# Differential attention: low parts of k in both halves of the rows, k in 512-token halves

## The chip, the cores and the metric

The kernel runs on one core of one Trainium2 chip. The time is device microseconds (us) of one execution; lower is better. The engines named below are TensorE (PE; its weight loads are listed apart as PEld), VectorE (DVE), ScalarE (ACT), GpSimd (POOL) and SyncE (SP, which issues DMAs).

## What is computed

Two blocks of two layers each on 1024 tokens with 1024 features, all in 32-bit floats. The change lies in the differential attention of the second block, which runs once per layer, so twice:

```python
q = q.reshape(B, S, DA_HEADS, 2, DA_QK_DIM).transpose(0, 2, 3, 1, 4)
k = k.reshape(B, S, DA_HEADS, 2, DA_QK_DIM).transpose(0, 2, 3, 1, 4)
...
s = jnp.einsum('bhmqd,bhmkd->bhmqk', q_blk, k).astype(jnp.float32) * scale
mask = kpos[None, :] <= qpos[:, None]
p = jax.nn.softmax(jnp.where(mask, s, -jnp.inf), axis=-1)
a = p[:, :, 0] - lam * p[:, :, 1]
return jnp.einsum('bhqk,bhkd->bhqd', a.astype(v.dtype), v)
```

There are 4 heads (DA_HEADS), each with two maps m of 64 features (DA_QK_DIM), and 8 query tiles of 128 tokens. Tile t sees the keys of tiles 0 to t.

## The kernel before, in words

**Products in parts.** A 32-bit operand is split into a high part (rounded to float32r) and a low part (the rest), and a product is the sum of high by high, low by high and high by low.

**The loop.** `diff_attention` (L1445) goes through n = 0 to 31, tile t = n % 8 of head n // 8. In one turn of the loop (L1607) the order on TensorE is written out and pinned: scores of map 0 of tile n; `values` of tile n-3 (L1572: weights times v); `transpose` of the first half of tile n-2 (L1561); `project` of q and k of tile n+3 (L1497: 24 products of 256 columns); scores of map 1 of tile n; `transpose` of the second half of tile n-2, if it has one; `turn` of tile n+2 (L1511: three transposes of q and k). The other engines take their instructions in an order that the scheduler sets when the program is built; each engine runs its own list strictly in that order.

**turn** puts the transposed, rotated q and k into SBUF. q of map m: high parts in rows 64 m and on, low parts in the other 64 rows (tile dq). k: high parts of both maps in both halves of the rows (tile dk, ScalarE, L1524). The low parts of k are in tile dkl, map m in rows 64 m (VectorE, L1529, two subtractions of 64x128). dk and dkl hold a head's 1024 tokens, with two buffers each.

**scores** (L1533) makes for each chunk of up to 512 keys two products with q of map m as weights: with dk over 128 rows, which sums high q by high k and low q by high k, and with dkl over the 64 rows of the map, high q by low k (L1547 and L1548). A last product of 128 columns adds the causal mask (weights and moving operand from the tile dccm, L1549). All score products of a map add up in one PSUM tile y of two buffers. VectorE then takes the negated maximum of each row (tile dnm, L1551), ScalarE the exponential (L1553), and after map 1 VectorE joins the two maps (L1555 to L1559).

**transpose and values.** The joined weights are turned by TensorE; ScalarE copies the high part, VectorE subtracts the low part (tiles dp, `split`, L191; one for the first four key tiles and one for the rest, one buffer each). `values` starts with the first dp tile; its ninth product is the first that reads the second one.

```python
1547  self.mm(sp[:, cs], q[:, m], kk[:, m, cs], start=True, stop=False)
1548  self.mm(sp[:, cs], q[r, m], kl[r, cs], start=False, stop=(c1 < W))
```

Every matrix product of the kernel is issued in the helper at L151 and every transposition by TensorE at L156, so the profile is read by tile names.

Of the kernel before, what the change touches and what calls it, by code (L numbers as in the profile page):

```python
# [12 lines left out]
F32 = mybir.dt.float32  # L13
F32R = mybir.dt.float32r
I32 = mybir.dt.int32
AF = mybir.ActivationFunctionType
OP = mybir.AluOpType
# [4 lines left out]
P = 128  # L22
# [75 lines left out]
class UT:  # L98
    """Transposed activations, split in two float32r parts: [feature, token]."""
# [12 lines left out]
class Pools:  # L112
    """Several pools, chosen by tag."""
# [8 lines left out]
class TagPool:  # L122
    """One pool per tag (a new pool waits only for the pools it overlaps); a tile without a tag is a tag of its own."""
# [18 lines left out]
class Kern:  # L142
# [30 lines left out]
    def psum(self, ctx, left="", right=""):  # L173
        """One PSUM pool per tag, stacked from either end."""
        for side, tags in (("left", left), ("right", right)):
            for t in tags:
                self.ps.tags[t] = self.pool(ctx, "ps" + t, space=PSUM, side=side)

    def pp(self, tag, bufs, shape=None):
        """PSUM tile; a tag of a phase always comes with the same bufs."""  # L180
        return self.ps.tile(shape or [P, 512], F32, tag=tag, bufs=bufs, name=self.nm(tag))
# [4 lines left out]
    def split(self, hi, lo, src, scale=None):  # L186
        """hi = float32r(src), lo = src - hi (src times scale), src in PSUM or SBUF."""
# [8 lines left out]
    def wsplit(self, hi, lo, raw, eng=None, cut=1, act=False):  # L196
        """Split, the high part on ScalarE if act; the low part in as many pieces as cut says (short ones delay other work
        of the engine less)."""
# [9 lines left out]
    def load_w(self, pool, w, c0, n, kts=KT, tag="w", bufs=None, dve=0, cut=1):  # L208
        """Weight columns c0..c0+n, split: w[kt][part] is [128, n]; every dve-th chunk on VectorE alone."""
# [15 lines left out]
    def next_w(self, c0, ahead=0):  # L225
        """The weight columns at c0 of the list in self.order, or those after them."""
# [7 lines left out]
    def gemm_T(self, w, ut, out, cols=slice(0, P)):  # L234
        """out [128 features, 1024 tokens] in PSUM, as two halves."""
        nc = self.nc
        for half in range(2):
            self.gemm_T_half(w, ut, half, out[half], cols)
# [7 lines left out]
    def gemm_N(self, ps, w, cols, lhs, kts=KT):  # L246
        """ps [128 tokens, features]; lhs(part, kt) is the stationary operand."""
# [7 lines left out]
    def transposes(self, dst, src, n):  # L255
        """dst [.., n, 128] = blocks of src [128, n * 128] transposed."""
# [3 lines left out]
    def to_T(self, src, ut, t):  # L260
        """src [128 tokens, 1024] in SBUF -> ut token tile t."""
# [6 lines left out]
    def rsqrt(self, y, v, pool, src=None, mul=1.0, eps=0.0):  # L268
        """y = v ** -0.5 (integer first guess, three Newton steps), v = src * mul + eps if src is given."""
# [20 lines left out]
    def silu2(self, out, src, tmp):  # L290
        """out = 2 silu(src) = src (1 + tanh(src / 2))."""
# [3 lines left out]
    def rms_rstd(self, src, n, eps, junk, pool):  # L295
        """[128, 1] = (mean(src ** 2) + eps) ** -0.5 over the free axis."""
# [13 lines left out]
    # ---------------------------------------------------------------- setup  # L310
# [11 lines left out]
    def transposed_columns(self, dst, rows_ap, nrow, pool):  # L322
        """dst [128, nrow] = rows_ap [nrow, 128] transposed."""
# [7 lines left out]
    # ---------------------------------------------------------------- first block, layer 0  # L331
    def phase_A(self, x_in):
        nc, i = self.nc, self.i
        with ExitStack() as ctx:
# [6 lines left out]
            with ExitStack() as c0:  # L341
# [23 lines left out]
                # relative position bias vectors, one row per head  # L365
# [11 lines left out]
                # shift and scale, one feature per partition  # L377
# [7 lines left out]
                # column c of block c: ones  # L385
# [69 lines left out]
            def fill(n):  # L455
                """PE work of the projections and gates, as many pieces."""
# [6 lines left out]
            def step(job, n):  # L463
                """The scores of job, with the rest of the one before it."""
# [42 lines left out]
    def dil_gate(self, lp, ut, w_in, hp, g, sgs):  # L507
        """2 silu(gate) of head pair hp of group g, transposed."""
# [13 lines left out]
    def dil_product(self, lp, hp, g, sgs, os, wtd, yT):  # L522
        """y^T rows of head pair hp of group g: attention times weight times gate."""
# [11 lines left out]
    def mod_jobs(self, lp, cs, jobs):  # L535
        """Thirds of silu(c) @ ada_w + ada_b of a layer, to DRAM, and the convolution taps by channel."""
# [63 lines left out]
    def dil_project(self, lp, ut, w_in, hp, g, res):  # L600
        """q, k, v of heads (2 hp, 2 hp + 1) of group g, tokens in the order of the group; v with tokens on
        partitions."""
# [30 lines left out]
        def split_q(q):  # L633
            """High parts of head a in rows 64 a, low parts in the others."""
# [8 lines left out]
        def split_k(k, low):  # L643
            """High parts of head a in both halves of the rows, low parts in rows 64 a."""
# [20 lines left out]
        # the second half of the tokens comes last in the very first group  # L665
# [13 lines left out]
    def dil_batches(self, lp, hp, g, tbd, std, qkv, os):  # L679
        """Unnormalised attention of heads (2 hp, 2 hp + 1) of group g -> os [2 heads x 64, token], as a list of  # L680
        batches."""
# [12 lines left out]
        class Head:  # L694
            def __init__(self, a):
# [7 lines left out]
                # batches of score tiles: rows, width, [(q0, k0, out position)], bias slices  # L703
# [24 lines left out]
            def finish(self):  # L728
                """Output row and row statistics, the latter to DRAM in token order."""
# [85 lines left out]
    def dil_weights(self, lp, hp, std, wtd):  # L815
        """exp(m_g - M) / sum_g s_g exp(m_g - M) per token, head, group."""
# [20 lines left out]
    # ---------------------------------------------------------------- first block, layer 1  # L837
    def rope_pairs(self, eng, a, b, cos, sin, pool, shp):
        """Rotate the pair (a, b) in place; cos and sin broadcast to shp."""
# [91 lines left out]
    def mla_heads(self, ctx, cr, lat, kbuf, rope, sgd, yT, rd, begin_tail):  # L931
# [60 lines left out]
        def scores(n):  # L992
            """exp(S - max) of query tile n % 8 of head n // 8."""
# [107 lines left out]
    def tail_weights(self, pool, w_out, kts, gate, eng, pin=False):  # L1101
        """Rows of w_out times the gate, split; eng multiplies."""
# [12 lines left out]
    def tail_begin(self, ctx, parts, w_out, layer, eng):  # L1115
        """First part of a tail, while the mixer still runs: the weights of its finished parts."""
# [8 lines left out]
    def tail_finish(self, ctx, early, late, w_out, x_res, layer):  # L1125
        """x = layernorm(alpha x + gate * (y @ w_out)); next layer's transposed input.

        Parts are the rows of y^T as [block, 128, token] views, in the order in which they are made."""
# [100 lines left out]
    # ---------------------------------------------------------------- second block, mixers  # L1229
    def phase_mix(self, l, ut, x_res):  # L1230
# [3 lines left out]
        with ExitStack() as ctx:  # L1234
# [35 lines left out]
            def end(early, n):  # L1270
                """Parts of the output product between the last tiles."""
# [12 lines left out]
    def pool_mixer(self, lp, us, pooled, sums, l, mixd):  # L1284
        """us [128 channels, 2, 1024 tokens]: windowed means minus us, times pool_w, to mixd."""
# [37 lines left out]
    def retention(self, lp, dp, wn, l, ut, w_in, mixd):  # L1323
        """Pool mixer and retention, to mixd; returns the last step of the latter, one tile at a time."""
# [120 lines left out]
    def diff_attention(self, dp, wn, l, ut, w_in, mixd, rest, late_pool, begin_tail, end, products):  # L1445
        """Differential attention of the four heads, one query tile after the other; the projections of q and k run
        LEAD tiles ahead."""
# [49 lines left out]
        def project(n):  # L1497
            """q and k of tile n % 8 of head n // 8, rotated."""
# [12 lines left out]
        def turn(n):  # L1511
            """Transposed and split. q: high parts of map m in rows 64 m, low parts in the others; k: high parts in both
            halves of the rows, low parts of map m in rows 64 m."""
            h, t = divmod(n, NT)
            c = raw_qk.pop(n)
            if t == 0:
                ks[h] = (lp.tile([P, 2, S], F32R, tag="dk", bufs=2, name=self.nm("dk")),
                         lp.tile([P, S], F32R, tag="dkl", bufs=2, name=self.nm("dkl")))
            kk, kl = ks[h]
# [3 lines left out]
            ts = slice(t * P, (t + 1) * P)  # L1523
# [4 lines left out]
            for m, r in enumerate(rows):  # L1528
                nc.vector.tensor_tensor(kl[r, ts], tp[r, 1 + m], kk[r, m, ts].bitcast(F32), OP.subtract)  # L1529
# [3 lines left out]
        def scores(n, m):  # L1533
            """exp(S_m - max); after both maps exp(S_0 - max) - lam z_0 / z_1 exp(S_1 - max), with the row sums z."""
            h, t = divmod(n, NT)
            W = (t + 1) * P
            q, (kk, kl) = qs[n], ks[h]
# [4 lines left out]
            r = slice(m * 64, (m + 1) * 64)  # L1542
# [375 lines left out]
```

## Time and profile before

| what | value |
|---|---|
| time, median of 3 runs | 4187.02 us (4184.1 to 4189.52) |
| span of the profiled execution, first to last instruction | 4168.8 us; its own total time is not listed apart |
| median less that span | 18.2 us |
| TensorE busy | 3945.4 us, 95% |
| weight loads busy | 3282.7 us, 79% |
| VectorE busy | 2430.4 us, 58% |
| ScalarE busy | 1371.7 us, 33% |
| GpSimd busy | 1087.9 us, 26% |
| the two attention loops, first scores to last maximum | 1776.8 to 1991.6 us and 3077.1 to 3291.9 us |

The profile is of one execution. Times within it are microseconds from the start of its span. A busy share over the whole span is a mean over stages with different limits, so the two attention loops are read by themselves. TensorE's products are pipelined and their ends are modelled, so that two neighbours can overlap in the list; what a product takes is read from one start to the next. Instructions on VectorE overlap a little in the same way.

### The profile page before, as it was taken

Reading aid. Unit: us, or ns where it says so; the run is one execution under the profiler, and the core shown is the slowest. Engines: PE = TensorE matmul, PEld = TensorE weight load, DVE = VectorE, ACT = ScalarE, POOL = GpSimd, SP = SyncE. Lnnn points to the kernel's source line nnn. Section 1 sums busy time; section 2 is a strip of 40 time slices with the busy share of each in tenths; the row PEclk is TensorE's granted clock in tenths of the full one; section 3 lists DMA queues with packets and bytes.
Section 4 is the critical chain, followed back from the end, with each engine's and each line's share of the span. In section 5 each row is a group of like instructions: output and inputs, shape, how many; then the busy total and the mean of one; then the engine's idle time right before and its main releaser. Section 6 shows DMA issues by size and latency. Waiting matters only on the chain. (4 is left out here: it accounts for less than half of the span.)

```text
span 4168.8 us, 54321 instructions
## 1 busy us (share of the span) xinstructions
PE 3945.4 (95%) x21085; PEld 3282.7 (79%) x21085; DVE 2430.4 (58%) x4606; ACT 1371.7 (33%) x2908; POOL 1087.9 (26%) x1016
## 2 busy tenths in 40 slices
PE   7989896899999889999999999997999999999998
PEld 5768775788888778988778888886988778888886
DVE  6545445947787767578753434438568764444436
ACT  3323331126777632255421111113235431111111
POOL 1111211410221322233133232324133222222233
PEclk9989998999999999999999999998999999999999
DMA  6363727320110243110421111113111231111112
GB/s 234 90 81 87 90 57 124 112 67 21 38 35 19 79 130 97 46 32 26 137 81 51 45 51 46 46 56 115 46 42 37 82 122 50 46 46 51 41 51 81
DMA packets 318896, 290.79 MB, mean 70 GB/s; under 512 B 70779, under 2 KB 273267, under 8 KB 318638
## 3 DMA queue, kind: packets, MB, share of 16 engines
q1 hardware_dynamic: 313362, 268.23, 23.8%
q10 hardware_dynamic: 5276, 19.08, 1.5%
q8 instruction: 167, 2.74, 0.3%
q14 instruction: 91, 0.75, 0.1%
HBM read 240.26 MB, written 51.72 MB: 70 GB/s over the span
## 5 line engine op out<-in xcount | busy, mean ns | idle before, releaser
L203 POOL TENSOR_TENSOR wl<-wr,wh 128x1024 fp32r<-128x1024 f32 (+1 forms) x253 | 497.9, 1977 | 1553.1 <-DVE wh L199 1458.8
L199 DVE CAST wh<-wr 128x1024 fp32r<-128x1024 f32 x222 | 180.2, 813 | 713.5 <-PE y L151 310.6
L151 PE MATMUL y<-uh_m,wl 128*128 128x512 f32 x1056 | 415.8, 394 | 4.7 <-DVE z L1643 4.2
L151 PE MATMUL y<-uh_m,wh 128*128 128x512 f32 x1056 | 418.6, 396 | 0.0
L151 PE MATMUL y<-ul_m,wh 128*128 128x512 f32 x1056 | 417.6, 395 | 0.0
L1796 ACT ACTIVATE cv<-y,cw 128x1024 f32<-128x1024 f32 x66 | 79.8, 1209 | 775.7 <-PE y L151 775.7
L151 PE MATMUL g<-uh_a,wl 128*128 128x512 f32 x568 | 234.8, 413 | 32.7 <-DVE sg L293 32.6
L151 PEld LDWEIGHTS y<-uh_m,wl 128*128 128x128 f32 x1056 | 198.2, 188 | 54.8 <-issue 4.6
L151 PEld LDWEIGHTS y<-uh_m,wh 128*128 128x128 f32 x1056 | 198.2, 188 | 48.2
L151 PEld LDWEIGHTS y<-ul_m,wh 128*128 128x128 f32 x1056 | 198.2, 188 | 47.5 <-DVE ul_m L191 0.9
L151 PE MATMUL g<-ul_a,wh 128*128 128x512 f32 x568 | 227.7, 401 | 0.5 <-POOL ul_a L422 0.4
L151 PE MATMUL g<-uh_a,wh 128*128 128x512 f32 x568 | 227.0, 400 | 0.0
L151 PE MATMUL y<-wo,yh 128*128 128x512 f32 x784 | 217.5, 400 | 2.7 <-ACT yh L1168 2.5
L191 DVE TENSOR_TENSOR pt<-t,pt 128x512 fp32r<-128x512 f32 x256 | 165.8, 680 | 21.9 <-ACT pt L190 21.0
L151 PEld LDWEIGHTS y<-wo,yh 128*128 128x128 f32 x784 | 147.7, 191 | 36.4 <-ACT yh L1168 4.3
L151 PE MATMUL y<-wl,hh 128*128 128x512 f32 x440 | 175.2, 398 | 0.0
L151 PE MATMUL y<-wh,hh 128*128 128x512 f32 x440 | 174.9, 398 | 0.0
L151 PE MATMUL y<-wh,hl 128*128 128x512 f32 x440 | 174.8, 397 | 0.0
L1005 DVE TENSOR_REDUCE nm<-s 128x1 f32<-128x1024 f32 x128 | 155.7, 1216 | 27.4 <-PE s L151 26.7
L151 PE MATMUL g<-wl,uh_n 128*128 128x256 f32 x576 | 166.2, 289 | 2.9 <-DVE dv L191 2.4
L151 PE MATMUL g<-wl,uh_f 128*128 128x256 f32 x576 | 166.0, 288 | 3.0 <-DVE dv L191 2.5
L151 PE MATMUL v<-pt,v 128*64 128x256 f32 (+1 forms) x1024 | 154.9, 294 | 10.2 <-DVE o L1040 10.2
(450 smaller groups left out, 10263.1 us busy)
## 6 DMA issues: line engine op xcount, KB each, us to landing
wr<-w_up SPq DMA_DIRECT2D x88, 512.0 KB
wr<-ada_w SPq DMA_DIRECT2D x48, 512.0 KB
wr<-w_down SPq DMA_DIRECT2D x44, 512.0 KB
wr<-a_w_in SPq DMA_DIRECT2D x36, 512.0 KB
wr<-w_in SPq DMA_DIRECT2D x24, 512.0 KB
xs<-wr SPq DMA_DIRECT2D x16, 512.0 KB
wr<-xs ACTq DMA_DIRECT2D x16, 512.0 KB
wr<-w_in SPq DMA_DIRECT2D x32, 256.0 KB
```

Source lines behind the costliest of these rows:

```text
L151: ins = self.nc.tensor.matmul(*args, **kw)
L191: nc.vector.tensor_tensor(lo, src, hi.bitcast(F32), OP.subtract)
L199: (self.nc.scalar.copy if act else self.nc.vector.tensor_copy)(hi, raw)
L203: (eng or self.nc.gpsimd).tensor_tensor(lo[..., cs], raw[..., cs], hi[..., cs].bitcast(F32), OP.subtract)
L1005: nc.vector.tensor_reduce(nm, sp, AX.X, OP.max, negate=True)
L1796: nc.scalar.activation(t, ps, AF.Identity, bias=cw[:, 3, c:c + 1], scale=cw[:, 2, c:c + 1])
```

## The change

The low parts of k are kept for both maps in both halves of the rows, as the high parts are. `turn` makes them with one subtraction of 128 rows by two maps by 128 tokens in place of two of 64x128. In `scores` the second product has 128 rows: it adds low q by low k to what was computed before. dk and dkl are split into halves of 512 tokens with three buffers each, in place of whole heads with two. Lines behind L1529 move up by two. Comments and docstrings that go are left out here.

```diff
 def turn(n):
     h, t = divmod(n, NT)
     c = raw_qk.pop(n)
-    if t == 0:
-        ks[h] = (lp.tile([P, 2, S], F32R, tag="dk", bufs=2, name=self.nm("dk")),
-                 lp.tile([P, S], F32R, tag="dkl", bufs=2, name=self.nm("dkl")))
-    kk, kl = ks[h]
+    if t % 4 == 0:
+        ks[h, t // 4] = [lp.tile([P, 2, 512], F32R, tag=x, bufs=3, name=self.nm(x)) for x in ("dk", "dkl")]
+    kk, kl = ks[h, t // 4]
...
-    ts = slice(t * P, (t + 1) * P)
+    ts = slice(t % 4 * P, (t % 4 + 1) * P)
     nc.scalar.copy(kk[:, :, ts], tp[:, 1:3])
...
-    for m, r in enumerate(rows):
-        nc.vector.tensor_tensor(kl[r, ts], tp[r, 1 + m], kk[r, m, ts].bitcast(F32), OP.subtract)
+    nc.vector.tensor_tensor(kl[:, :, ts], tp[:, 1:3], kk[:, :, ts].bitcast(F32), OP.subtract)
...
 def scores(n, m):
...
-    q, (kk, kl) = qs[n], ks[h]
+    q = qs[n]
...
-    r = slice(m * 64, (m + 1) * 64)
...
-        self.mm(sp[:, cs], q[:, m], kk[:, m, cs], start=True, stop=False)
-        self.mm(sp[:, cs], q[r, m], kl[r, cs], start=False, stop=(c1 < W))
+        kk, kl = ks[h, c0 // 512]
+        self.mm(sp[:, cs], q[:, m], kk[:, m, :c1 - c0], start=True, stop=False)
+        self.mm(sp[:, cs], q[:, m], kl[:, m, :c1 - c0], start=False, stop=(c1 < W))
```

The built programs have the same instructions on TensorE and SyncE, in the same order. On VectorE the list is rearranged by a few places. The first place is the stretch around the second maximum of tile 6 of the second head and the low part of the second dp tile of tile 4 behind it, which `values` of tile 4 reads (dnm: negated maxima; drr and rs: the norm of four finished tiles; dq: low parts of q). Before:

```order
L287 SCALAR_TENSOR_TENSOR rs_18585<-rs_18585,dss_18064 128x4
L1551 TENSOR_REDUCE dnm_18426<-y_18420 128x1
L191 TENSOR_TENSOR dp_18435<-t_18436,dp_18434 128x128
L1529 TENSOR_TENSOR dkl_18441<-t_18443,dk_18440 64x128 x2
L1531 TENSOR_TENSOR dq_18442<-t_18443,dq_18442 64x128 x2
L1555 RECIPROCAL drs_18349<-dsm_18348 128x2
L1551 TENSOR_REDUCE dnm_18462<-y_18456 128x1
```

With the change:

```order
L288 SCALAR_TENSOR_TENSOR drr_18569<-rs_18571,drr_18569 128x4
L1549 TENSOR_REDUCE dnm_18414<-y_18408 128x1
L191 TENSOR_TENSOR dp_18423<-t_18424,dp_18422 128x128
L1527 TENSOR_TENSOR dkl_18429<-t_18431,dk_18428 128x2x128
L1529 TENSOR_TENSOR dq_18430<-t_18431,dq_18430 64x128 x2
L1549 TENSOR_REDUCE dnm_18449<-y_18443 128x1
L1553 RECIPROCAL drs_18337<-dsm_18336 128x2
```

One short instruction of the norm (drr) now stands ahead of the maximum (dnm); the two subtractions for dkl have become one; and the next maximum stands ahead of the reciprocal (drs).

The second place is the next tile of the same head: the second maximum of tile 7 and the low part of the second dp tile of tile 5 (do with dcgs: the norm again). Before:

```order
L191 TENSOR_TENSOR dp_18484<-t_18485,dp_18483 128x512
L1601 SCALAR_TENSOR_TENSOR do_18063<-do_18063,drr_18583,dcgs 128x128 x2
L1551 TENSOR_REDUCE dnm_18556<-y_18550 128x1
L191 TENSOR_TENSOR dp_18565<-t_18566,dp_18564 128x256
L1529 TENSOR_TENSOR dkl_18441<-t_18572,dk_18440 64x128 x2
L1531 TENSOR_TENSOR dq_18571<-t_18572,dq_18571 64x128 x2
```

With the change:

```order
L191 TENSOR_TENSOR dp_18471<-t_18472,dp_18470 128x512
L1599 SCALAR_TENSOR_TENSOR do_18054<-do_18054,drr_18569,dcgs 128x128 x2
L1549 TENSOR_REDUCE dnm_18543<-y_18537 128x1
L191 TENSOR_TENSOR dp_18552<-t_18553,dp_18551 128x256
L1527 TENSOR_TENSOR dkl_18429<-t_18559,dk_18428 128x2x128
L1529 TENSOR_TENSOR dq_18558<-t_18559,dq_18558 64x128 x2
```

The places of the maximum and of the dp tile behind it are the same; only the dkl row differs.

## Rows read from the trace of the kernel before

**Rows 1.** Busy time of each engine (number of instructions), granted clock, DMA; one head, one layer's loop.

```profile
1827.16:1884.04 56.88, 56.88 (x391) 47.88 (x390) 45.78 (x131) 33.74 (x109) 18.74 (x57) 1.00 0.10 29
1776.80:1991.60 214.80, 214.33 (x1436) 177.79 (x1434) 171.61 (x483) 128.71 (x412) 74.52 (x213) 1.00 0.09 27
```

**Rows 2.** All instructions on tile dkl: durations in ns, first and last start, shapes.

```profile
L151 PE MATMUL y<-dkl,dq x192: 322/466/502, 1777.0 to 3289.8; 64*128 64x512 f32 x96, 64*128 64x128 f32 x32, 64*128 64x256 f32 x32, 64*128 64x384 f32 x32
L1529 DVE TENSOR_TENSOR dkl<-t,dk x128: 259/290/298, 1774.9 to 3281.9; 64x128 fp32r<-64x128 f32 x128
```

**Rows 3.** PE in order of time, scores of three tiles: start us, us, instruction.

```profile
1859.98 0.48 PE L151 MATMUL y<-dk,dq 128*128 128x512 f32 x1
1860.39 0.50 PE L151 MATMUL y<-dkl,dq 64*128 64x512 f32 x1
1860.83 0.39 PE L151 MATMUL y<-dk,dq 128*128 128x256 f32 x1
1861.14 0.38 PE L151 MATMUL y<-dkl,dq 64*128 64x256 f32 x1
1861.45 0.33 PE L151 MATMUL y<-dccm 128*128 128x128 f32 x1
1861.62 0.91 PE L151 MATMUL g<-dv,dp 128*128 128x256 f32 x6
...
1873.43 0.40 PE L151 MATMUL y<-dk,dq 128*128 128x512 f32 x1
...
1874.18 0.45 PE L151 MATMUL y<-dk,dq 128*128 128x384 f32 x1
...
1884.04 0.31 PE L151 MATMUL y<-dk,dq 128*128 128x128 f32 x1
...
1884.53 0.33 PE L151 MATMUL y<-dccm 128*128 128x128 f32 x1
1884.69 1.60 PE L151 MATMUL g<-dv,dp 128*128 128x256 f32 x12
```

**Rows 4.** Weight loads in order of time, a projection, then scores.

```profile
1871.06 0.19 PEld L151 LDWEIGHTS g<-wh,ul_n 128*128 128x128 f32 x1
1871.18 0.19 PEld L151 LDWEIGHTS g<-wl,uh_n 128*128 128x128 f32 x1
...
1873.75 0.18 PEld L151 LDWEIGHTS y<-dkl,dq 64*128 64x128 f32 x1 [0.25 <-issue]
```

**Rows 5.** PE in order of time, elsewhere: 96-row products, transposes, 512-column products.

```profile
1005.88 0.63 PE L151 MATMUL s<-kb,qh 96*128 96x512 f32 x2
1006.35 1.04 PE L156 MATMUL t<-ident,pe 128*128 128x128 f32 x8
1007.14 1.18 PE L151 MATMUL v<-pt,v 128*128 128x256 f32 x8
...
2110.22 0.40 PE L151 MATMUL y<-uh_m,wl 128*128 128x512 f32 x1
2110.45 0.39 PE L151 MATMUL y<-uh_m,wh 128*128 128x512 f32 x1
```

**Rows 6.** VectorE's waits from 1840.8 to 1885.3 us: total, times, longest.

```profile
DVE dnm L1551 <- PE y L151: 3.9, 4, 1.2
```

**Rows 7.** VectorE in order of time, the two ends of that stretch.

```profile
1840.32 0.42 DVE L1551 TENSOR_REDUCE dnm<-y 128x1 f32<-128x256 f32 x1 [2.14 <-PE y L151]
...
1884.89 0.41 DVE L191 TENSOR_TENSOR dp<-t,dp 128x256 fp32r<-128x256 f32 x1
```

**Rows 8.** VectorE by shape before the loop: a subtraction of 128x256 from PSUM.

```profile
L191 DVE TENSOR_TENSOR dv<-g,dv 128x256 fp32r<-128x256 f32 x16 | 6.7, 419 | 16.4 <-ACT dv L190 16.3
```

**Rows 9.** VectorE's waits from 1973.6 to 1991.7 us, the end of the loop.

```profile
DVE dkl L1529 <- ACT dq L1527: 0.4, 1, 0.4
```

**Rows 10.** Busy time around a drop of the granted clock, columns as in rows 1.

```profile
1725.00:1737.00 12.00, 9.94 (x83) 9.73 (x83) 11.66 (x36) 1.49 (x4) 6.89 (x9) 1.00 0.10 35
1737.00:1740.40 3.40, 3.40 (x18) 3.40 (x17) 3.40 (x10) 0.00 (x0) 2.63 (x5) 0.50 0.22 73
```

## The prediction

> **What bounds the kernel now.** I read the busy time by stretches first. In one head of the attention loop (56.88 us, tile 0 to tile 0) TensorE is busy all the time at clock 1.00, VectorE for 45.78 us, ScalarE for 33.74 and GpSimd for 18.74; a whole loop looks the same, TensorE 214.33 of 214.80 us [rows 1]. So TensorE sets the pace, but VectorE is not far behind: that is what the reader should keep in mind. The second view is the list of what touches dkl: 192 products of 64 rows (96 of 512 columns, 32 each of 384, 256 and 128) and 128 subtractions on VectorE of about 290 ns [rows 2]. The third is TensorE in order of time around the scores, where steps are read from start to start. In tile 5 the first product of 512 columns gives way after 0.41 us, its 64-row partner after 0.44; the pair of 256 columns takes 0.31 and 0.31, the mask product 0.17 [rows 3]. Elsewhere a step of 512 columns is 0.23 us, and 96-row products are followed by transposes without such a loss (2 of 512 columns in 0.47) [rows 5]. In a projection of 256 columns weight loads begin 0.12 us apart, while the load for the 64-row product starts only after an idle 0.25 us [rows 4]. I read this as a price of about 0.2 us for each change between 128 and 64 rows: the running product has to drain before the next weights are loaded.
>
> **What the change does to TensorE.** The number of products and their columns stay, but all have 128 rows. Steps after it, from other rows: 512 columns 0.232 us (0.23 in rows 5, 0.235 from the two 96-row products); 256 columns 0.12 [rows 4]; 384 columns 0.175, the middle of these (an estimate); 128 columns 0.10, from 8 transposes in 0.79 us [rows 5]. The shortest a 128-column step could be is half the 256-column one, 0.06.
>
> - 512: a pair takes 0.85 us as in tile 5, and 0.75 where the scores follow a projection (1873.43 to 1874.18) [rows 3]; mean 0.80, after it 0.464: saves 0.336 x 96 = 32.3 us.
> - 384: from the neighbours 0.74 (an estimate between 0.85 and 0.62), after it 0.35: 0.39 x 32 = 12.5.
> - 256: 0.62 - 0.235 = 0.385 x 32 = 12.3.
> - 128: 0.49 (1884.04 to 1884.53 [rows 3]) - 0.20 = 0.29 x 32 = 9.3.
> - the mask product, 128 times: 0.16 - 0.10 = 0.06: 7.7.
>
> Sum 74 us, or 9.3 per head and layer. With 0.06 for 128 columns it would be 85; without any gain in how products overlap it would be 0. I take 74, since the rows that set it come from the same loop or the same kind of product.
>
> **What it does to VectorE.** Two subtractions of 64x128 (0.29 us each, 0.59 together) become one of 128x256. Before the loop one of that size from PSUM takes 0.419 us [rows 8]. So each of the 64 turns gives back 0.17 to 0.2 us (I take 0.2), 1.6 per head.
>
> **How much of the 74 us comes out.** VectorE must then keep up. I follow one stretch of the second head, from the second maximum of tile 1 at 1840.32, which VectorE takes up the moment TensorE is ready, to the low part of the second dp tile of tile 5, from 1884.89 to 1885.30 [rows 7]: 44.98 us. In it VectorE waits 3.9 us for TensorE [rows 6]; all else is its own work or waits for ScalarE, which I leave in. With six turns less 0.2 it needs 44.98 - 3.9 - 1.2 = 39.9 us if it never waits for TensorE again. TensorE wants this dp tile at the ninth product of the `values` that begin at 1884.69: twelve products to the next group, 0.12 us each, so at 1885.65 [rows 3], 45.37 us after 1840.28, the end of those scores. Off that comes the saving of tiles 2 to 7 and of tile 0's first map. By the steps above the two maps of tiles 2 to 7 save 0.8, 0.8, 1.4, 1.6, 1.6 and 1.6 us and the last one 0.35: 8.1. TensorE needs 37.3. So it has to wait **2.6 us per head** for VectorE, near the end of the heavy tiles; in tiles 0 and 1, where VectorE has long waits for TensorE (2.14 us before 1840.32 alone [rows 7]), the debt is paid back. Where a head follows: three times in a layer, 7.8 us, two layers 15.6.
>
> The end of the loop has no projections left, and VectorE has no wait for TensorE from 1973.6 to 1991.7 us [rows 9]: it is the bound already. There tiles 5 to 7 save 4.7 us on TensorE, of which only VectorE's own 0.4 (two turns) comes out, and VectorE arrives about 1 us late (an estimate: a part of the 2.6). That takes off 5.3 per layer, 10.6 in all. Left: 74 - 15.6 - 10.6 = 48 us.
>
> **The rest costs nothing.** Each half buffer holds 512 tokens; the next write into one comes three tiles after its last reader (head h's first half is last read by tile 7 and rewritten when head h+1 turns tile 4, which happens beside tile 2's scores). If that cover went, one ScalarE copy would wait and the scores two tiles later with it. SBUF use is equal: 16 + 8 KB a row before, 12 + 12 after. SyncE's list is the same. On GpSimd a quarter of a weight split moves ahead of the last rotation step; the turn that reads it comes a whole tile (about 7 us) later, and GpSimd is busy for 18.74 of 56.88 us [rows 1]. The moves on VectorE put one short norm step ahead of a maximum: no work added.
>
> **The sum.** The span is 4168.8 us; the median of the runs is 4187.02, 18.2 above, which I take as what lies around the span. 4187 - 48 = **4139 us**.
>
> **Rivals.**
> 1. VectorE keeps up after all (its list has slack that my account counts as work): all 74 us come out, 4113. For it: in tiles 0 and 1 it waits long. Against: rows 9, where it is the bound already. Chance 0.13; likely values 4108 to 4125.
> 2. VectorE's waits don't shrink: its list is strictly in order, so that behind each maximum it waits for a ScalarE copy or a transpose, and TensorE then waits for dp and for PSUM in each tile. Only the 64 x 0.2 = 13 us of removed work come out: 4174. Against: its waits for TensorE in the heavy tiles are few and long, 4 in 3.9 us [rows 6], and these close by themselves. Chance 0.15, values between 4155 and 4174.
> 3. Weight loads for products on the same 128 rows can't run beside a product: each score step stays at about 0.43 us, the VectorE gain is hidden, and the time is 4187. Rows 4 speak against it: loads of 0.19 us start 0.12 us apart beside products on the same rows. The Trainium skill, TensorE: Matmul & The Clock Gate, Part 3 (The mechanism), says that a weight load overlaps a running matmul only when the row group differs; by that rule this rival would hold, and this trace does not agree. Chance 0.05.
> 4. Slower: TensorE's clock drops. In this trace one stop of TensorE for about 2 us before 1737 (busy 9.94 of 12 us) is followed by 3.4 us at 0.50, that is 1.2 in place of 2.4 GHz [rows 10], which loses 1.7 us. My forecast has stops of that size. It is slower than before once more than 48 / 1.7 = 28 of the 64 tiles bring one; with all 64, 109 us are lost: 4248. Against: two stops a head would cost 16 x 1.7 = 27, and the time would be 4166, still faster. Chance 0.05.
>
> **Chances and range.** My forecast has 0.62, with a range of its own from 4126 to 4155. The range 4112 to 4166 takes in most of the first two rivals and leaves out less than 0.2. A measurement of this kernel can tell about 0.2%, 8 us, from no change. Faster 0.62 + 0.13 + 0.15 = 0.90; the same 0.05; slower 0.05.
>
> **What would show it.** After the change the dkl rows have 128 rows, steps of 0.23 us in place of 0.43, and no idle of the weight loads between them; the loop is some 24 us shorter per layer; VectorE's waits for TensorE in the heavy tiles are near zero and TensorE's waits for dp about 2 to 3 us per head, named with tiles 4 to 7. Wrong would be: steps that stay above 0.3 us (rival 3), no wait for dp (rival 1), waits in the light tiles too (rival 2), or a granted clock below 1.00 in the loop (rival 4).

## The result and the profile after

| what | before | with the change |
|---|---|---|
| time, median | 4185.83 us (4184.1 to 4189.52) | 4132.24 us (4131.64 to 4134.16) |
| ratio | | 0.9866, interval 0.9853 to 0.9879 |
| profiled execution: its time, its span | span 4168.8 | 4134.16, span 4132.4 |
| up to the first scores of the first loop | 1776.8 | 1790.9 |
| loop 1, first scores to last maximum | 214.80 | 189.16 |
| between the loops | 1085.5 | 1086.5 |
| loop 2 | 214.81 | 189.21 |
| after loop 2 | 876.9 | 876.6 |

The change saves 53.6 us, 1.3%; 48 were forecast. As far as the two profiles can tell, it is in the two loops, which give 25.6 us each, 51.2 together; the stretches behind each loop agree within 1 us, and the other 2.4 us are less than the runs of the kernel before differ among themselves. The stretch up to the first loop, where both programs do the same work, takes 14 us longer in the second profile. It also differs between two profiles of the changed kernel alone (1790.9 and 1777.6 us), so whole times are compared as ratios to the kernel before on the same chip, and stages by their own length.

Busy time with the change, for the second head (first scores of tile 0 to those of the next head) and for the first loop, columns as in [rows 1]:

```profile
1833.40:1883.15 49.75, 48.56 (x391) 46.73 (x390) 44.00 (x123) 32.90 (x108) 18.84 (x58) 1.00 0.11 33
1790.90:1980.06 189.16, 182.31 (x1436) 173.69 (x1434) 165.07 (x453) 125.68 (x412) 75.33 (x213) 1.00 0.10 31
```

The head has gone from 56.88 to 49.75 us with the same 391 products, at the same clock of 1.00. TensorE is no longer busy all the time: in the loop 6.85 us are idle, 0.47 before. VectorE has 6.54 us less to do in the loop (171.61 before), 0.20 for each of its 32 turns.

All instructions on tile dkl, as in [rows 2]:

```profile
L151 PE MATMUL y<-dkl,dq x192: 272/364/398, 1791.0 to 3253.0; 128*128 128x512 f32 x96, 128*128 128x128 f32 x32, 128*128 128x256 f32 x32, 128*128 128x384 f32 x32
L1527 DVE TENSOR_TENSOR dkl<-t,dk x64: 396/415/425, 1789.0 to 3245.6; 128x256 fp32r<-128x256 f32 x64
```

Still 192 products, now of 128 rows, and 64 subtractions of 415 ns in place of 128 of 290. TensorE in order of time: the second map of tile 5 (a projection ends ahead of it), before and with the change, then three places at which TensorE waits (in brackets the idle time before the row and what ended it). Before:

```profile
1865.61 0.40 PE L151 MATMUL y<-dk,dq 128*128 128x512 f32 x1
1865.94 0.49 PE L151 MATMUL y<-dkl,dq 64*128 64x512 f32 x1
1866.36 0.39 PE L151 MATMUL y<-dk,dq 128*128 128x256 f32 x1
1866.68 0.38 PE L151 MATMUL y<-dkl,dq 64*128 64x256 f32 x1
1866.99 0.33 PE L151 MATMUL y<-dccm 128*128 128x128 f32 x1
1867.15 0.52 PE L156 MATMUL t<-ident,dc 128*128 128x128 f32 x3
```

With the change:

```profile
1867.47 0.39 PE L151 MATMUL y<-dk,dq 128*128 128x512 f32 x1
1867.70 0.40 PE L151 MATMUL y<-dkl,dq 128*128 128x512 f32 x1
1867.94 0.28 PE L151 MATMUL y<-dk,dq 128*128 128x256 f32 x1
1868.05 0.28 PE L151 MATMUL y<-dkl,dq 128*128 128x256 f32 x1
1868.17 0.23 PE L151 MATMUL y<-dccm 128*128 128x128 f32 x1
1868.23 0.51 PE L156 MATMUL t<-ident,dc 128*128 128x128 f32 x3
...
1883.52 1.14 PE L151 MATMUL g<-dv,dp 128*128 128x256 f32 x8
1884.86 0.73 PE L151 MATMUL g<-dv,dp 128*128 128x128 f32 x4 [0.20 <-DVE dp L191]
...
1928.35 0.50 PE L151 MATMUL g<-dv,dp 128*128 128x128 f32 x2 [0.65 <-DVE dp L191]
...
1967.24 0.55 PE L156 MATMUL t<-ident,dc 128*128 128x128 f32 x3 [0.77 <-POOL dc L846]
```

From start to start the steps are 0.23, 0.24, 0.11, 0.12 and 0.06 us, together 0.76; the same five products took 1.54. (The group in [rows 3] is the first map's: 1.64 us before and 0.84 now.) The weight loads, in order of time, show the same:

```profile
1867.47 0.19 PEld L151 LDWEIGHTS y<-dkl,dq 128*128 128x128 f32 x1
1867.70 0.19 PEld L151 LDWEIGHTS y<-dk,dq 128*128 128x128 f32 x1
1867.94 0.19 PEld L151 LDWEIGHTS y<-dkl,dq 128*128 128x128 f32 x1
1868.06 0.19 PEld L151 LDWEIGHTS y<-dccm 128*128 128x128 f32 x1
```

The idle quarter of a microsecond that stood ahead of the 64-row load [rows 4] is gone; the load for each product starts as the product before it does, or close to it. Before, the load for the 64 rows began at 1873.75 us, 0.32 behind the start of a product that is 0.40 us long [rows 3, rows 4]. The mask product (dccm) has weights of its own and loses nothing here, so what is gone is the price of other rows and not of other weights.

What TensorE now waits for in the first loop (total, times, longest):

```profile
PE g L151 <- DVE dp L191: 3.1, 9, 0.7
PE t L156 <- POOL dc L846: 1.3, 2, 0.8
PE y L151 <- ACT de L1551: 1.1, 3, 0.5
PE t L156 <- DVE dp L191: 0.6, 3, 0.2
PE t L156 <- DVE dq L1529: 0.5, 3, 0.2
```

The kernel before has one row in this view of its loop, a wait of 0.4 us for ScalarE. The first row is the forecast one: `values` waits for the low part of a dp tile. The three places in the list above are read as follows. At 1884.86 it is the ninth product of the `values` of tile 5 that waits, after eight products, as the prediction has it. At 1928.35 VectorE shows why, in its own order of time:

```profile
1926.93 0.16 DVE L288 SCALAR_TENSOR_TENSOR drr<-rs,drr 128x4 f32<-128x4 f32 x1
1927.02 1.08 DVE L1549 TENSOR_REDUCE dnm<-y 128x1 f32<-128x896 f32 x1
1928.02 0.28 DVE L191 TENSOR_TENSOR dp<-t,dp 128x128 fp32r<-128x128 f32 x1
```

VectorE never idles here: the short steps of the norm and the maximum of tile 6 stand ahead of the dp tile in its list, and that one ends at 1928.30, when TensorE goes on. The stretch of VectorE that the prediction followed [rows 7] has these ends now:

```profile
1845.59 0.42 DVE L1549 TENSOR_REDUCE dnm<-y 128x1 f32<-128x256 f32 x1 [1.75 <-PE y L151]
...
1884.39 0.41 DVE L191 TENSOR_TENSOR dp<-t,dp 128x256 fp32r<-128x256 f32 x1
```

From the first start to the end of the second row (1884.80) it takes 39.2 us, and behind its first row VectorE waits for TensorE not once.

The last of the three places is one that the prediction did not count. GpSimd in order of time:

```profile
1963.22 1.81 POOL L203 TENSOR_TENSOR wl<-wr,wh 128x256 fp32r<-128x256 f32 x2 [3.29 <-DVE wh L199]
...
1965.97 0.73 POOL L203 TENSOR_TENSOR wl<-wr,wh 128x256 fp32r<-128x256 f32 x1
1966.66 0.28 POOL L845 TENSOR_TENSOR dc<-rp,rp 128x48 f32<-128x48 f32 x1
1966.90 0.28 POOL L846 TENSOR_TENSOR dc<-rp,rp 128x48 f32<-128x48 f32 x1
```

Pieces of a weight split, two ahead of the rotation and one ahead of its last two steps, make the turn's transposes wait 0.77 us.

### The profile page after: what moved, and what is told of

It reads as the page before. It is cut to its first block, busy times and chain, and to the rows that moved or that the text cites. A ratio compares the mean times of both kernels' runs of the same rounds, so it can differ in the third digit from the quotient of the medians.

```text
span 4132.4 us, 54251 instructions
## 1 busy us (share of the span) xinstructions
PE 3887.2 (94%) x21085; PEld 3281.0 (79%) x21085; DVE 2416.1 (58%) x4542; ACT 1364.7 (33%) x2908; POOL 1089.5 (26%) x1016
## 5 line engine op out<-in xcount | busy, mean ns | idle before, releaser
L151 PE MATMUL v<-pt,v 128*64 128x256 f32 (+1 forms) x1024 | 154.5, 294 | 10.9 <-DVE o L1040 10.8
```

The source lines that it names most:

```text
L151: ins = self.nc.tensor.matmul(*args, **kw)
```

## The experiments

Four theories were to be told apart. **Drain**: each change between 64 and 128 rows costs TensorE about 0.2 us, and the gain is that these changes go. **The rest of the change**: the lighter subtraction, the third buffer or the halves bring it. For what stays behind (72 us less for TensorE, 51 less in time): **VectorE's amount of work** or **its order**. In the table, the ratio is to the kernel before on the same chip, and the loops are first scores to last maximum.

| run | time, us | ratio, interval | loop 1, loop 2 |
|---|---|---|---|
| e1_rows64 | 4168.32 | 0.9987, 0.9977 to 0.9997 | 214.14, 214.19 |
| e2_grouped | 4147.99 | 0.9938, 0.9923 to 0.9953 | 204.76, 204.76 |
| e3_dve_more | 4143.46 | 0.9926, 0.9912 to 0.9941 | 199.32, 200.03 |
| e4_norm_off | 4133.39 | 0.9905, 0.9890 to 0.9919 | 191.69, 189.60 |
| after_again (the changed kernel) | 4120.00 | 0.9872, 0.9857 to 0.9887 | 189.36, 189.50 |
| e5_dil_turned | 4107.82 | 0.9846, 0.9829 to 0.9862 | 189.14, 189.29 |
| e6_norm_pool | 4117.81 | 0.9868, 0.9853 to 0.9883 | 192.85, 186.84 |
| e7_swap | 4115.77 | 0.9863, 0.9849 to 0.9878 | 187.91, 187.77 |
| e8_both | 4105.25 | 0.9833, 0.9812 to 0.9853 | 187.98, 187.97 |
| e9_no_norm | 4117.98 (one run) | none | 187.33, 187.37 |

The times expected for e1 to e4 were worked out from the first measurement (4187 us); on the chip of these four the kernel before takes 4173.58. As they stand, e1, e2 and e3 lie below their ranges (e3 by 1.5 us); by ratio to 4185.83 they are 4180, 4160 and 4155 us, in the range or at its edge. e4 lies in the range of its rival as it stands, and by ratio, at 4146 us, above both of its ranges.

The changed kernel run again gives the same ratio within its interval (0.9872) and loops within 0.3 us. What was expected of it:

> The changed kernel as it is, beside the others on one chip. Its two loops are 189.2 us each as in its first trace (214.8 before), and the ratio to the kernel before is 0.986 to 0.988, whatever the first block takes on this chip.

**e1: the changed kernel with products of 64 rows.** Buffers, halves and the single subtraction stay; the second product uses 64 rows again.

```diff
-                self.mm(sp[:, cs], q[:, m], kl[:, m, :c1 - c0], start=False, stop=(c1 < W))
+                r = slice(m * 64, (m + 1) * 64)
+                self.mm(sp[:, cs], q[r, m], kl[r, m, :c1 - c0], start=False, stop=(c1 < W))
```

> The changed kernel, but its second score product reads only the 64 rows of its map again (halves, three buffers and the wide subtraction for dkl stay). Theory (each change between 128 and 64 rows drains TensorE): the steps of 0.3 to 0.44 us come back, TensorE sets the pace again, each loop is 212 to 215 us and the time 4178 to 4187, since the lighter subtractions are hidden. Rival (the gain came from the halves or from VectorE's lighter turn): the time stays within 10 us of 4132.

The loops are 214.14 and 214.19 us, 0.65 shorter than before the change, and the products have their old durations again (instructions on dkl; compare [rows 2]):

```profile
L151 PE MATMUL y<-dkl,dq x192: 322/466/502, 1775.7 to 3288.1; 64*128 64x512 f32 x96, 64*128 64x128 f32 x32, 64*128 64x256 f32 x32, 64*128 64x384 f32 x32
```

So without the 128 rows of the product 25 of the 25.6 us of a loop are gone; all other parts of the change, by themselves, bring some 0.65. The lighter subtraction is worth almost nothing while TensorE is the bound; with 128 rows it counts, as e3 shows.

**e2: the kernel before with fewer changes.** Where there are two chunks (tiles 4 to 7), both dk products go first, then both dkl products of 64 rows: two changes of rows in a group in place of four, the same products.

```diff
-            for c0 in range(0, W, 512):
-                c1 = min(W, c0 + 512)
-                cs = slice(c0, c1)
+            chunks = [(slice(c0, min(W, c0 + 512)), min(W, c0 + 512)) for c0 in range(0, W, 512)]
+            for cs, c1 in chunks:
                 self.mm(sp[:, cs], q[:, m], kk[:, m, cs], start=True, stop=False)
+            for cs, c1 in chunks:
                 self.mm(sp[:, cs], q[r, m], kl[r, cs], start=False, stop=(c1 < W))
```

> The kernel before, but in tiles 4 to 7 both 128-row products of a map come first and then both 64-row products, so that a group has two changes of rows and not four; nothing else moves. Theory (the price is the change, about 0.2 us each): the second of two neighbouring 64-row products takes 0.23 us, each of the 64 groups is some 0.4 us shorter, 25 us in all, of which a few stay in VectorE's waits: 4160 to 4170. Rival (a 64-row product is slow by itself, 0.43 us whatever its neighbours): 4184 to 4188.

Each loop gets 10.0 us shorter. TensorE in order of time, a group of the same five products as in the list of the changed kernel above:

```profile
1855.67 0.39 PE L151 MATMUL y<-dk,dq 128*128 128x512 f32 x1
1855.90 0.28 PE L151 MATMUL y<-dk,dq 128*128 128x256 f32 x1
1856.11 0.49 PE L151 MATMUL y<-dkl,dq 64*128 64x512 f32 x1
1856.44 0.28 PE L151 MATMUL y<-dkl,dq 64*128 64x256 f32 x1
1856.65 0.33 PE L151 MATMUL y<-dccm 128*128 128x128 f32 x1
1856.81 0.30 PE L156 MATMUL t<-ident,dc 128*128 128x128 f32 x1
```

The two dk products take 0.44 us (0.35 in the changed kernel: 0.23 and 0.12), the dkl products 0.33 and 0.21 (0.24 and 0.12), the mask 0.16 (0.06): 1.14 together, where four changes need 1.54 and none 0.76, in the same place of tile 5. The step ahead of a change is 0.1 us longer than its like, and so is the one behind it: half of a price lies on each side. There are 64 such groups, 12 of them where VectorE is the bound already; 20.1 us over the other 52 is 0.39 for a group and two changes, or **0.19 us for one**, against the 0.2 of the prediction. The change takes away 384 changes of rows, two in a group of tiles 0 to 3 and four in one of tiles 4 to 7; at 0.19 us these are 73 us. (Of the 25.6 us of the whole time, 5.5 are outside the loops, most in the unchanged first stretch, 1771.0 us here and 1775.4 in e1; this stretch varies by itself.)

**e3: more work for VectorE.** The subtraction for dkl in the changed kernel is issued twice, 0.415 us more in each turn, 13.3 in a loop.

```diff
             nc.vector.tensor_tensor(kl[:, :, ts], tp[:, 1:3], kk[:, :, ts].bitcast(F32), OP.subtract)
+            nc.vector.tensor_tensor(kl[:, :, ts], tp[:, 1:3], kk[:, :, ts].bitcast(F32), OP.subtract)
```

> The changed kernel with the subtraction for dkl done twice: 64 more instructions of about 0.42 us on VectorE, 27 us, and no work for TensorE. Theory (VectorE sets the pace from tile 2 to 7 and at the end of the loop): about six of eight turns come out, 13 to 22 us: 4145 to 4155, and TensorE's waits for dp grow. Rival (TensorE still sets the pace, its waits for VectorE are incidental): 4130 to 4137.

The loops grow by 10.0 and 10.5 us, three quarters of what was added, and TensorE's waits in the first loop are for VectorE (the longest two of three rows):

```profile
PE t L156 <- DVE dq L1530: 9.3, 9, 2.2
PE g L151 <- DVE dp L191: 6.1, 7, 1.3
```

So VectorE is the next bound in most of the loop. (dq stands behind the doubled subtraction in its list, which is why this row leads.)

**e4 and e6: the norm's last step on other engines.** If VectorE's amount of work sets the pace, four of its instructions for each four tiles elsewhere should help. e4 gives the step to ScalarE and GpSimd:

```diff
-                    nc.vector.scalar_tensor_tensor(oa[:, j], oa[:, j], rr[:, j:j + 1], gs, OP.mult, OP.mult)
+                    nc.scalar.mul(oa[:, j], oa[:, j], rr[:, j:j + 1])
+                nc.gpsimd.tensor_tensor(oa, oa, gs[:, None, :].to_broadcast([P, 4, P]), OP.mult)
```

> The changed kernel with the last step of the norm of four tiles taken off VectorE: 64 instructions of 0.36 us, 23 us in both layers, become 64 on ScalarE and 16 on GpSimd. Theory (VectorE sets the pace in the heavy tiles): TensorE's waits for dp (5.0 us in a layer's loop) fall below 3 us and the end of the loop is shorter, 5 to 14 us less: 4118 to 4127. Rival (TensorE sets the pace, or ScalarE's added work delays as much): 4130 to 4136.

It failed: a ratio of 0.9905 against 0.9872 for the changed kernel, 14 us more, loops no shorter (191.69 and 189.60 us), and the stretches after them longer (1092.6 and 881.5 us against 1086.0 and 876.9). Behind the first loop TensorE has a wait that the changed kernel does not have:

```profile
PE g L156 <- DMA wr<-mixd: 4.6, 1, 4.6
```

TensorE waits there for finished heads to be read back, and GpSimd's list shows why they are late. For the first four tiles of the last head, ScalarE's part of the step ends at 1971.84 us. GpSimd's multiplication behind it stands behind a weight split of 2.40 us and ends at 1975.45:

```profile
1973.70 1.75 POOL L1600 TENSOR_TENSOR do<-do,dcgs 128x512 f32<-128x512 f32 x1
```

In the second trace of the changed kernel VectorE's four instructions end at 1970.28. The 5.0 us that this expectation and that of e7 name as waits for dp in a loop take in one of 1.9 us behind it; inside the loop they are 3.7 (3.1 and 0.6 above). e6 gives the step to GpSimd alone:

```diff
-                for j in range(4):
-                    nc.vector.scalar_tensor_tensor(oa[:, j], oa[:, j], rr[:, j:j + 1], gs, OP.mult, OP.mult)
+                nc.gpsimd.tensor_tensor(oa, oa, rr[:, :, None].to_broadcast([P, 4, P]), OP.mult)
+                nc.gpsimd.tensor_tensor(oa, oa, gs[:, None, :].to_broadcast([P, 4, P]), OP.mult)
```

> The changed kernel with the last step of the norm on GpSimd alone (two instructions for four tiles in place of four on VectorE), nothing added to ScalarE. Theory (VectorE sets the pace, and the run before gained nothing because ScalarE's list, in order, held up the copies that VectorE waits for): loops of 183 to 187.5 us, 3 to 12 us less in all. Rival (VectorE's total work doesn't matter in this place, only what stands ahead of the low part of the second dp tile): loops of 188.5 to 190 us.

Loop 2 is 2.7 us shorter, loop 1 3.5 longer, with a single wait of 3.4 us for dq in it. The whole time is that of the changed kernel within the intervals. What made that wait stands in the trace: ahead of dq, VectorE's joining of the two maps of tile 3 takes 2.85 us, and beside it GpSimd is in a weight split.

```profile
1889.65 2.85 DVE L1557 SCALAR_TENSOR_TENSOR de<-de,drs,de 128x384 f32<-128x384 f32 x1
1889.75 2.34 POOL L203 TENSOR_TENSOR wo<-wm,wo 128x1024 fp32r<-128x1024 f32 x1
```

All 16 joinings of this shape take 0.61 or 0.62 us in the changed kernel; in e6 ten of them do, five take 1.32 or 1.33 and this one 2.85. That GpSimd's work is the reason is read from these times and was not tested by itself. With it in the way, e6 does not tell VectorE's amount of work from its order.

**e9: that step left out.** The output is then not normalised.

```diff
-                for j in range(4):
-                    nc.vector.scalar_tensor_tensor(oa[:, j], oa[:, j], rr[:, j:j + 1], gs, OP.mult, OP.mult)
```

> The changed kernel without the last step of the norm: the differential attention's output is not divided by its root mean square and not multiplied by the gain. 32 instructions of 0.36 us, 11.5 us a layer, leave VectorE and go nowhere. Theory (VectorE's total work in the heavy tiles sets the pace): of the 11.5 us some 3 to 6 come out of each loop, 183 to 186.5 us, and TensorE's waits for dp fall by half. Rival (only what stands ahead of the low part of the second dp tile counts): 187.5 to 189.5 us.

Loops of 187.33 and 187.37: neither range held them, and the one for the order of VectorE's list missed by less than 0.2. In the first loop VectorE is busy for 3.85 us less (161.43 against 165.28 in the second trace of the changed kernel), and 2.0 us come out. The 3.85 are far from 11.5: only 24 of the 32 instructions (8.7 us) lie ahead of the loop's last maximum, neighbours of the list overlap, and other instructions take longer. The longest two rows of TensorE's waits that are left:

```profile
PE g L151 <- DVE dp L191: 3.0, 6, 0.7
PE t L156 <- DVE dq L1529: 1.4, 1, 1.4
```

Less work leaves the waits for dp at 3.0 us, where they should have halved. The single wait for dq is e6's again: a short instruction on VectorE (drs, 128x1) takes 1.66 us where 0.21 is usual, from 1889.72 to 1891.38, while GpSimd's weight split runs from 1888.96 to 1891.36; loop 2 has the like. Without this wait the loops would be near 186.0 us (an estimate, 187.33 less 1.35), in the range of the amount of work. So e9 speaks for the amount, but does not settle it.

**e7: another order on TensorE.** The transposition of the second half goes ahead of the second scores, so that the dp tile can be made earlier; no work is added or taken away.

```diff
-            if 0 <= n < NQ:
-                scores(n, 1)
...
+            if 0 <= n < NQ:
+                scores(n, 1)
```

> The changed kernel with the transposes of the second half of tile n-2 ahead of the scores of map 1 of tile n, so that on VectorE the low part of the second dp tile comes before that map's maximum. No work is added or taken away. Theory A (TensorE's waits are for this one row behind the maximum): its waits for dp fall from 5.0 us in a layer's loop to below 2, loops of 185 to 187.5 us, 4 to 8 us less in all. Theory B (VectorE's total work sets the pace, the wait only shows up where it is asked for): the waits move to the turn or to the scores, and the loops stay within 1 us of 189.2.

The loops are 1.5 and 1.7 us shorter than in the changed kernel, between the two expectations. TensorE's waits in the first loop:

```profile
PE t L156 <- DVE dp L191: 2.6, 6, 0.8
PE t L156 <- POOL dc L846: 1.3, 2, 0.8
PE y L151 <- ACT de L1551: 1.2, 3, 0.6
PE g L151 <- DVE dp L191: 1.0, 3, 0.7
PE t L156 <- DVE dq L1529: 0.7, 3, 0.4
```

The waits of `values` for dp fall from 3.1 to 1.0 us, but transpositions wait 2.6 in place of 0.6: nearly all of the listed wait has found a new place. TensorE's idle time is the same, 6.9 us against 7.0, so the gain of 1.6 us is in its busy time, in steps that got shorter without a wait in the list. A wait that comes from VectorE's pace moves along the list when the order changes.

**e5 and e8: the same price elsewhere.** In the dilated attention of the first block a product of 128 rows and one of 64 alternate as well. e5 turns every second pair around, so that equal rows meet:

```diff
-                        kern.mm(sp[:rows, j, :], qa, ka, start=True, stop=False)
-                        kern.mm(sp[:rows, j, :], qa[rs], low, start=False, stop=True)
+                        for n, (x, y) in enumerate(((qa, ka), (qa[rs], low))[::1 - j % 2 * 2]):
+                            kern.mm(sp[:rows, j, :], x, y, start=(n == 0), stop=(n == 1))
```

> The changed kernel; in the dilated attention of the first block, whose low score products still have 64 rows, every second tile of a batch makes its 64-row product first, so that two 64-row products stand side by side and a batch of two tiles has two changes of rows and not four. Theory (about 0.2 us for each change): some 54 batches give 0.4 us each, 20 us of TensorE's time, of which 8 to 20 come out, as TensorE waits for VectorE there at few places: 0.9815 to 0.985 of before, the loops of the second block unchanged. Rival (that stage is bound by VectorE's chain, or the price is that of a 64-row product): no more than 4 us less than the changed kernel.

The stretch up to the first loop falls from 1777.6 to 1763.8 us, and the whole time by 12, from 4120.00 to 4107.82; the loops stay. Counted in the traces, changes to and from 64 rows fall from 228 to 144; 84 at 0.19 us are 16 us, of which 13.8 come out. Here the two neighbouring 64-row products have different weights, and the gain is there all the same. e8 has the edits of e5 and e7:

> The turned order of products in the first block's dilated attention and the earlier transposes of the second half, both on top of the changed kernel. They lie in different stages, so the gains should add: 14 us less in the first block and 1.5 us less in each loop (187.8), 16 us in all: 0.982 to 0.9845 of before. If one takes room from the other (VectorE's list is set anew as a whole), the time stays near that of the better one, 0.9845 to 0.986.

Both gains add: 1764.6 us up to the first loop, loops of 188.0, 4105.25 us in all. At 0.9833 of the kernel before it is 16 us (0.4%) below the changed kernel by the two ratios. Against e5 alone the whole times do not decide, as the intervals overlap; the lengths of the stages do.

## Why the prediction was right, and where its sizes were off

- **TensorE's saving, forecast 74 us: 72 measured.** From the first product of a group of scores to the next instruction behind it, taken as the median for each tile and map over its 8 groups (those with a wait behind them left out), the 128 groups need 155.4 us before and 83.3 after. Part of the good fit is luck. The steps of 512 and 256 columns are as forecast (0.23, 0.12), but the first product behind the transpositions still takes 0.32 us for 512 columns, which the forecast did not count: products of 512, 384 and 256 columns save 29.4, 10.8 and 10.9 us in place of 32.3, 12.5 and 12.3. The mask step was put at 0.10 us and is 0.06 in most tiles: it saves 11.7 in place of 7.7. The two nearly cancel. (The 85 us that the prediction gives for steps of 0.06 would be 82 by its own terms.)
- **The cause, a price at each change of rows: shown** by e1 (undone by the 64 rows alone) and e2 (0.19 us a change without any of the edit). That the price is a drain is how the late loads of [rows 4] are read, where the ends of products are modelled. The Trainium skill, TensorEngine Tiling (Array Packing), Tiling Modes (Key Properties), says that changing the tiling mode, not just the tile, drains TensorE. These runs agree with it, at 0.19 us for each change between 64 and 128 rows.
- **VectorE then holds TensorE up, forecast 26.2 us (15.6 in the heads, 10.6 at the end): about 21.** By the 72 us a head saves 9.0. The three full heads of the first loop give 7.9 (50.36 to 42.50), 7.1 (56.88 to 49.75) and 6.2 (56.87 to 50.64), the last one up to the last maximum 4.4 (50.70 to 46.26): 1.2, 1.9, 2.8 and 4.6 us stay behind, 10.5 a loop against 13.1 forecast; some of it is GpSimd's, as told below. The price of 2.6 us a head was too high. In the stretch of the second head that the prediction followed, VectorE never waits for TensorE, as forecast, but it needs 39.2 us and not 39.9: this 0.7 is the difference between 2.6 and the 1.9 that this head loses. 0.5 of it are waits for ScalarE, which fell from 1.5 to 1.0 us. The first head was charged what was worked out for the second, and loses less. The end was charged 5.3 and costs 4.6; from 1963.4 us to the last maximum VectorE has no wait at all in this view, where [rows 9] have one of 0.4 us, for ScalarE.
- **Its place.** The waits stand at the low part of the second dp tile, as forecast, but the longest, 0.62 to 0.65 us, at the ninth product of tile 4, as at 1928.35 above; that of tile 5 has 0.2, and transpositions have the rest. The listed waits of the second head come to 1.4 us (1.2 from its first product on), while 1.9 stay behind. A wait costs more than its idle time: from start to start, the four steps of this head with a wait in them, and the steps behind them, take 2.1 us longer than their likes without one.
- **GpSimd, forecast at nothing: listed waits of 1.3 us a loop.** The sentence that failed is that the turn which reads the rotation comes a whole tile (about 7 us) later. At the end of the loop it came 5.3 us behind ScalarE's copies that the rotation waits for (1972.81 to 1978.07) before the change, and without its wait would come 3.5 behind them now (1962.94 to 1966.47). Twice in a loop a weight split ahead of the rotation on GpSimd then makes TensorE wait. The longer of the two waits begins with VectorE: the split waits 3.29 us for VectorE's part of the weight (wh) before it starts. The other one, 0.53 us in the third head, makes its steps 0.8 us longer, nearly all of the 0.9 by which that head loses more than the second; so VectorE's part is about 2 us in both.
- **The base.** The 18.2 us were taken as lying around the span, but in the profiled run after only 1.8 us do. The rest is likely the first stretch, which took 14 us longer in the profile after; no profile of the kernel before at 4187 us shows it. The difference forecast was not touched by this.
- **The sum.** 72 - 21 = 51 us, the two loops; the time is 6.8 us below the forecast and in its own range. Both larger terms were too high, the saving by 2 us and the waits by 5.
- **The rivals.** That VectorE keeps up (74 us out) fell by the waits for dp and by e3. That its waits do not shrink fell: in the stretch of [rows 6], which now begins at 1845.59, VectorE's waits for TensorE went from 3.9 us in four to none. That equal rows cannot overlap their loads fell with the steps of 0.23 us. The Trainium skill, TensorE: Matmul & The Clock Gate, Part 3 (The mechanism), says that a weight load overlaps a running matmul only when the row group differs. By that rule the time would have stayed; the loads of 0.19 us beside running products of the same 128 rows do not agree with it. That the clock drops fell: it is 1.00 in both loops. But TensorE's stops in them are 0.8 us at most, so that stops of 2 us, which this rival was about, did not come.

What stays open: how much of the 10.5 us a loop is VectorE's amount of work and how much its order. e3 returned three quarters of the time added, e7 gained 1.6 us by order alone, and in e6 and e9 VectorE's instructions beside GpSimd's took longer. Both count, and how much each was not separated.

## What to carry to other kernels

When two kinds of product alternate, read the step from start to start at each seam. Here an idle time of the weight loads at a change of rows was a price of the seam, and it went where the small product was filled up to the rows of its neighbour, or where equal ones were put side by side. Then ask at once how much of the saving the next engine can follow, head by head and not from one head for all: here 72 us of TensorE's time became 51. Giving an engine's work to others with strictly ordered lists can cost more than it frees (e4), and VectorE's own instructions may take longer beside the added work (e6).

## What was not expected of the hardware

- A change of rows is paid on both sides of it, 0.1 us in the step ahead and 0.1 in the one behind (e2). And a 128-column product steps in 0.06 us, half of a 256-column one, where 0.10 was taken from the transpositions.
- Single VectorE instructions took much longer while GpSimd worked: 2.85 in place of 0.61 us beside a weight split of 2.34 (e6), and 1.66 in place of 0.21 beside one of 2.40 (e9).
- The changed kernel differs by 12 us between its two measurements (4132.24 and 4120.00), nearly all of it in the stretch up to the first loop (1790.9 and 1777.6 us), while its loops agree within 0.3 us. Three of TensorE's waits in that stretch make 10 of the 13 us: 12.27, 10.95 and 27.35 us in the first profile, 9.21, 7.91 and 23.50 in the second. The record names a chip for the second measurement only, so that the cause is open. A whole time from one measurement set against a profile from another can mislead by half the gain of a loop.
